# Projections dealt beside the attention in steps of six products, and one weight cast placed behind the first scores

## The chip, the cores and the metric

The kernel runs on one core of one Trainium2 chip. The metric is the device time of one launch in microseconds (us), lower is better. A core has TensorE (PE in the profile, its weight loads PEld), VectorE (DVE), ScalarE (ACT), GpSimd (POOL) and SyncE (SP), which here issues most of the DMAs. Each engine works through its own queue in order, and semaphores join them.

## The reference

One decoder layer over 1024 tokens of width 1024, with 16 learned tokens ahead of them: a feed-forward half step, a mixer with two groups of heads (HGRN2, a gated recurrence, and stick-breaking attention), an output projection, and a second feed-forward half step. All is float32. Cut to what the change touches:

```python
u = rms_norm(h, mix_norm[l]) @ w_in[l]          # 3584 columns
hq, hf, hi, hg, sq, sk, sv = split(u)           # 4 x 512 for HGRN2, 3 x 512 for attention
o_hg = hgrn2(hq, hf, hi, hg, lb, out_gain, valid)
o_sb = stick_breaking(sq, sk, sv, q_gain, k_gain, valid)
h = h + concat([o_hg, o_sb]) @ w_out[l]
# stick_breaking, 8 heads of width 64, blocks of 128 queries, z = q.k / 8:
#   w[t, s] = sigmoid(z_ts) * prod over s < j < t of (1 - sigmoid(z_tj));  out = w @ v
```

## The kernel before, in words

The program has four stages in time: the first feed-forward half (to about 690 us of the trace), the mixer (690 to 1300), the second feed-forward half, and its output. The change lies within the mixer, in the stage that runs the attention, 851 to 1117 us. Every product with a weight is made of three matmuls (lines 249 to 251, tile `proj`): activations and weights are split into a rounded high part and a rest (`xh`, `xl`, `wh`, `wl`), and high times high, high times rest and rest times high are summed. A weight tile `raw` is loaded by a DMA on SP (line 227), cast into `wh` on ACT (line 232), and subtracted into `wl` on DVE (line 234). The raw tiles have two buffers, `wh` and `wl` three each.

The order of TensorE's instructions in this stage is the order in which the Python code emits them. The other engines' order is found by a scheduler from that code and from costs of its own; where the code says `issue_after(x)`, an instruction stands behind `x`.

**The attention** is cut into 32 jobs (8 heads, four pairs of query blocks each, in the order 0, 6, 2, 4), and `braid` gives each job a slot. A job has three kinds of steps. *Scores*, in its own slot: two matmuls (1665, 1666) fill a PSUM tile `z`; ACT makes `keep` and `sig` from it (1667, 1668), DVE runs the product scan over `keep` (1671) and POOL multiplies it into `sig` (1678). *Turns*, two slots later: TensorE transposes `sig` into PSUM tiles `flip` (1515, and 1571 for the meta tokens); ACT casts them into `wu` or `wm` (1643) and DVE subtracts the rest (1644). *Values*, three slots later: pairs of matmuls (1592, 1594) sum into `oacc`. `z` and `flip` have two PSUM banks each, so the third tile of a kind waits until the first is read.

**The fill.** For each slot `braid` adds up the estimated time of the attention steps in it, times 1.22, and draws so much from `hgrn_fill`: the projections of the HGRN2 heads. These go by columns, four per head: v, f, q, g (value, forget gate, query, output gate). v and f are made in four pieces of 256 or 272 tokens, q and g in two of 512. A piece fills one PSUM bank with 24 products, in two steps of twelve. In this stage the fill has one bank alone, the other being lent to a tile `begin` that the scans read. So the first product of a piece waits until the piece before has been read: v by one ACT copy (1148), f by two ACT sigmoids (1154, 1155), q and g by an ACT sigmoid (1162) and a DVE multiply (1163), into staging tiles `st` that have four buffers and are stored by SP.

The weight tile of the next column is loaded and split when the first step of a column is emitted. The first column in this stage is the query of head 0, and with its first step the tile of head 0's output gates is loaded, cast and subtracted. Sixteen steps of the fill (v and f of head 0) run ahead of the stage, 76 in it, and the last four (output gates of head 3) behind it.

Of the kernel before, what the change touches and what calls it, by code (L numbers as in the profile page):

```python
# [15 lines left out]
AF = mybir.ActivationFunctionType  # L16
# [4 lines left out]
P = 128  # L21
D = 1024
KT = D // P
# [26 lines left out]
class Block:  # L50
# [161 lines left out]
            (dst[3], lambda r: kept(3, sub, r[0], r[1])),  # L212
        ]

    def split_w(self, view, parts=None):
        nc = self.nc
        n = int(np.prod(view.shape[1:]))
        if parts is not None:
            got = []
            for i, tag in enumerate(self.w_tags):  # L220
                t = self.wp.tile([P, n], F32R, tag=tag, name="w" + "hl"[i], bufs=self.w_bufs)
                self.last_load = nc.sync.dma_start(t.bitcast(F32), parts[:, i])
                got.append(t)
# [3 lines left out]
        self.last_load = nc.sync.dma_start(to, view)  # L227
        hi = self.wp.tile([P, n], F32R, tag="wh", name="wh", bufs=self.w_bufs)
        if self.split_on_vector:
            nc.vector.tensor_copy(hi, raw)  # L230
        else:
            self.rounded = nc.scalar.copy(hi, raw)
        lo = self.wp.tile([P, n], F32R, tag="wl", name="wl", bufs=self.w_bufs)
        nc.vector.tensor_sub(lo, raw, hi.bitcast(F32))
        return hi, lo

    def col_tile(self, w, col):
        return self.split_w(
            w[:, col : col + P].rearrange("(k p) f -> p k f", p=P), self.parted.get(col)
        )  # L240

    def product(self, ps, w, xh, xl, c0, n, ks=None):
# [888 lines left out]
    def hgrn_fill(self, xh, xl, pool, dst):  # L1131

        nc = self.nc
        plan, cols = self.heads_plan, self.columns_of_heads()
        self.stores, self.level_banks = [], "zo"

        def staged(n):
            return pool.tile([P, 512], F32, tag="st", name="st", bufs=4)[:, :n]

        def use(kind, h, ps, c0, n):  # L1140
            s = slice(c0, c0 + n) if kind in "vf" else slice(c0 - META, c0 - META + n)
            t = staged(n)
            if c0 >= HALVES[1][0] and kind != "g":
                ps = ps[:, ::-1]
                at = s.start + HALVES[1][0] + T - 2 * c0 - n
                s = slice(at, at + n)
            if kind == "v":
                nc.scalar.copy(t, ps)
                with self.tc.issue_after(self.last_load.ins):
                    nc.sync.dma_start(dst[kind][h, :, s], t)  # L1150
                return
            elif kind == "f":
                k = staged(n)
                nc.scalar.activation(t, ps, AF.Sigmoid)
# [5 lines left out]
                nc.sync.dma_start(dst["k"][h, :, s], k)  # L1160
            else:
                nc.scalar.activation(t, ps, AF.Sigmoid)
                nc.vector.tensor_mul(t, t, ps)
            store = lambda: nc.sync.dma_start(dst[kind][h, :, s], t)
            if (kind, h) == plan[-1] and c0 == HALVES[1][0]:
                self.stores.append(store)
            else:
                store()

        kept = {}  # L1170

        def part(i, ci, c0, n, half):
            if ci == 0 and half == 0:
                kept["w"] = self.ahead_w.pop(cols[i])
                for c in cols[i + 1 : i + (3 if i == 0 else 2)]:
                    if c not in self.ahead_w:
                        self.ahead_w[c] = self.col_tile(self.a["w_in"][0], c)
                kept["round"] = self.rounds[cols[1]]
            if half == 0:
                kept["ps"] = self.proj_bank(n)  # L1180
            self.product(
                kept["ps"], kept["w"], xh, xl, c0, n, range(4 * half, 4 * half + 4)
            )
            if half == 1:
                with self.tc.issue_after(kept["round"]) if i == 0 else ExitStack():
                    use(*plan[i], kept["ps"], c0, n)

        for i, (kind, _) in enumerate(plan):
            for ci, (c0, n) in enumerate(PIECES if kind in "vf" else HALVES):
                for half in range(2):  # L1190
                    yield 12 * (n * 0.42 + 13), lambda a=(i, ci, c0, n, half): part(*a)

    def level_bank(self, shape, name):
        self.level_banks = self.level_banks[::-1]
# [451 lines left out]
    def sb_scores(self, pool, qs, ks, b, sigs):  # L1646
        nc = self.nc
        nk = META + P * (b + 1)
        pieces = -(-nk // 512)
        size = -(-nk // pieces)  # L1650
        size += size % 2
        q = qs[:, b * P : (b + 1) * P]
        kept = []

        def piece(s0, n):
            last = s0 + n == nk
            if last:
# [7 lines left out]
            nc.tensor.matmul(z, q, ks[0][:, s0 : s0 + n], start=True, stop=False)  # L1665
            nc.tensor.matmul(z, q, ks[1][:, s0 : s0 + n], start=False, stop=True)
            nc.scalar.activation(keep[:, s0 : s0 + n], z, AF.Sigmoid, scale=-1.0)
            nc.scalar.activation(sig[:, s0 : s0 + n], z, AF.Sigmoid)
            first, end = max(s0, 1), nk + 1 if last else s0 + n
            kv = keep[:, first:end][:, ::-1]  # L1670
            nc.vector.tensor_tensor_scan(
                out=kv, data0=kv, data1=self.begin[:, : end - first] if last
                else self.begin[:, :1].broadcast_to([P, end - first]),
                initial=0.0 if last else keep[:, end : end + 1],
                op0=ALU.mult, op1=ALU.max if last else ALU.bypass,
            )
            if s0 == 0:
                nc.gpsimd.tensor_mul(sig, sig, keep[:, 1 : nk + 1])
# [40 lines left out]
    def braid(self, jobs, fill, share, turn, value):  # L1719


        waiting = []
        owed = 0.0
        at = 0
        while True:
            job = next(jobs, None)
            for lag, steps in zip((0.0, turn, value), job or ()):
                spans = [1.0 if lag == turn else t for t, _ in steps]
                done = 0.0
                for span, (t, f) in zip(spans, steps):  # L1730
                    waiting.append((at + lag + (done + span / 2) / sum(spans), t, f))
                    done += span
            if not waiting:
                break
            now = [x for x in waiting if x[0] < at + 1]
            waiting = [x for x in waiting if x[0] >= at + 1]
            owed += share * sum(t for _, t, _ in now)
            more = []
            while owed > 0:
                step = next(fill, None)  # L1740
                if step is None:
                    break
                more.append(step)
                owed -= step[0]
            now += [(at + (i + 0.5) / len(more), t, f) for i, (t, f) in enumerate(more)]
            for _, _, f in sorted(now, key=lambda x: x[0]):
                f()
            at += 1
# [51 lines left out]
    def run(self):  # L1800
        nc, tc, a = self.nc, self.tc, self.a
# [20 lines left out]
        with ExitStack() as c0:  # L1822
            with ExitStack() as c1:
# [372 lines left out]
                with tc.manual_schedule(engines={nc.tensor.engine}):  # L2196
# [7 lines left out]
                    with ExitStack() as c2:  # L2204
# [216 lines left out]
```

## Time and profile before

| | |
|---|---|
| median of 3 runs | 1938.81 us (1938.69 to 1940.38) |
| the profiled execution's own time | 1938.33 us |
| span of its trace | 1936.6 us |
| DVE busy over the span | 1394.2 us (72%) |
| ACT busy over the span | 847.4 us (44%) |
| POOL busy over the span | 451.4 us (23%) |

The time of the profiled execution and its span differ by 1.73 us, which lies around the trace. A row of the timeline has the start in us, the duration, the engine, the line, the operation, the tile written and the tiles read, the shape, and in brackets the engine's idle time ahead of the instruction with what ended it. Matmuls are pipelined: a row's duration runs over into the next one, so the distance from one start to the next is the cost of a matmul.

### The profile page before, as it was taken

The numbers are of one execution on the slowest core, as the hardware profiler recorded it, in microseconds if no ns is written. First come the engines' busy times: TensorE is split into PE (matmuls) and PEld (weight loads), VectorE is DVE, ScalarE is ACT, GpSimd is POOL, SyncE is SP. The second block draws the span as 40 slices with busy tenths as digits, with TensorE's granted clock in tenths as the row PEclk, the third lists the DMA queues.
The fourth block names the chain that finished last, engine by engine and source line by source line (L and its number), as shares of the span: only waits on it lengthen the run. The fifth ranks groups of instructions, "written<-read, shape, count | busy, mean of one in ns | idle before, by whom it ended". The sixth has DMA issues, their size and how long they took to land.

```text
span 1936.6 us, 30253 instructions
## 1 busy us (share of the span) xinstructions
PE 1915.8 (99%) x10637; PEld 1620.7 (84%) x10637; DVE 1394.2 (72%) x2184; ACT 847.4 (44%) x1712; POOL 451.4 (23%) x625
## 2 busy tenths in 40 slices
PE   9999999999999999999999999999999999999999
PEld 7888888888888888889998988888888888888887
DVE  7977778877678665567777776667577767766774
ACT  7523343334444545356666635433223332344443
POOL 3010100101000003133333342210545544530000
PEclk9999999999999999999999999999999999999999
DMA  7266788757975416765454178646544444479473
GB/s 220 89 175 169 244 280 257 232 199 272 382 238 183 138 42 154 188 182 150 135 155 123 57 267 246 154 185 211 170 128 133 135 127 134 128 251 315 147 233 114
DMA packets 381687, 355.54 MB, mean 184 GB/s; under 512 B 129040, under 2 KB 284560, under 8 KB 381536
## 3 DMA queue, kind: packets, MB, share of 16 engines
q1 hardware_dynamic: 360768, 288.98, 49.3%
q0 software_dynamic: 20768, 64.63, 9.6%
q8 instruction: 84, 1.38, 0.3%
q14 instruction: 67, 0.55, 0.1%
HBM read 237.95 MB, written 115.57 MB: 183 GB/s over the span
## 4 chain that ended last, share of the span: by engine, by line
PE 92%; DVE 3%; DMA 2%; ACT 1%; issue 1%; SPq 0%; POOL 0%; DVEq 0%; POOLq 0%; ACTq 0%
PE o L735 22%; PE qb L452 18%; PE qc L452 12%; PE qa L452 12%; PE proj L249 5%; PE proj L251 5%; PE proj L250 5%; PE flip L1515 2%; PE wo L250 1%; PE wo L251 1%; PE wo L249 1%; PE mq L1014 1%; PE oacc L1594 1%; PE oacc L1592 1%; PE z L1665 1%
## 5 line engine op out<-in xcount | busy, mean ns | idle before, releaser
L452 PE MATMUL qb<-T,wh 128*128 128x512 f32 x1056 | 343.7, 390 | 1.4 <-DVE u L484 1.4
L452 PEld LDWEIGHTS qb<-T,wh 128*128 128x128 f32 x1056 | 198.2, 188 | 45.8 <-issue 3.5
L452 PE MATMUL qa<-B,wh 128*128 128x512 f32 x696 | 227.6, 392 | 0.3 <-ACT B L838 0.2
L362 DVE TENSOR_TENSOR wl<-s,wh 128x512 fp32r<-128x512 f32 x160 | 165.8, 1036 | 69.1 <-ACT wh L360 68.2
L249 PE MATMUL proj<-xh,wh 128*128 128x512 f32 (+2 forms) x640 | 212.7, 332 | 1.1 <-ACT kT L1391 0.6
L735 PE MATMUL o<-t,w 128*128 128x512 f32 x924 | 212.1, 390 | 0.0
L251 PE MATMUL proj<-xl,wh 128*128 128x512 f32 (+2 forms) x640 | 209.3, 327 | 0.7 <-DVE xl L1984 0.7
L735 PE MATMUL o<-parts 128*128 128x512 f32 x924 | 209.6, 389 | 0.0
L250 PE MATMUL proj<-xh,wl 128*128 128x512 f32 (+2 forms) x640 | 208.9, 326 | 0.0
L452 PE MATMUL qb<-T,wl 128*128 128x512 f32 x528 | 205.6, 389 | 0.0
L735 PEld LDWEIGHTS o<-t,w 128*128 128x128 f32 x924 | 172.8, 188 | 37.1 <-issue 0.8
L735 PEld LDWEIGHTS o<-parts 128*128 128x128 f32 x924 | 173.5, 188 | 36.0
L360 ACT CAST wh<-s 128x512 fp32r<-128x512 f32 x160 | 99.5, 622 | 186.6 <-PE qb L452 141.6
L452 PEld LDWEIGHTS qa<-B,wh 128*128 128x128 f32 x696 | 130.5, 188 | 29.2 <-issue 1.0
L360 ACT CAST wh<-raw 128x512 fp32r<-128x512 f32 x120 | 74.4, 621 | 143.2 <-PE qc L452 101.3
L452 PE MATMUL qa<-B,wl 128*128 128x512 f32 x348 | 135.5, 389 | 0.0
L249 PEld LDWEIGHTS proj<-xh,wh 128*128 128x128 f32 x640 | 120.9, 189 | 12.7 <-ACT st L1155 1.2
L251 PEld LDWEIGHTS proj<-xl,wh 128*128 128x128 f32 x640 | 120.9, 189 | 11.8 <-DVE xl L1984 1.2
L250 PEld LDWEIGHTS proj<-xh,wl 128*128 128x128 f32 x640 | 121.1, 189 | 9.2
L452 PEld LDWEIGHTS qb<-T,wl 128*128 128x128 f32 x528 | 99.1, 188 | 20.3
L452 PE MATMUL qc<-T,wh 128*128 128x512 f32 x352 | 115.9, 391 | 0.0
L452 PE MATMUL qc<-B,wh 128*128 128x512 f32 x352 | 114.6, 389 | 0.0
(400 smaller groups left out, 3832.5 us busy)
## 6 DMA issues: line engine op xcount, KB each, us to landing
raw<-in_ffn_w_in_dram SPq DMA_DIRECT2D x176, 256.0 KB, 3.9
raw<-in_ffn_w_out_dram SPq DMA_DIRECT2D x112, 256.0 KB, 4.5
w2in<-both SPq DMA_DIRECT2D x28, 512.0 KB, 4.0
raw<-in_w_in_dram SPq DMA_DIRECT2D x25, 512.0 KB, 4.3
ks<-kD SPq DMA_DIRECT2D x32, 260.0 KB, 4.8
wout<-both SPq DMA_DIRECT2D x16, 512.0 KB, 3.9
wh<-w2in SPq DMA_DIRECT2D x27, 256.0 KB, 3.1
wl<-w2in SPq DMA_DIRECT2D x27, 256.0 KB, 3.3
```

Source lines behind the costliest of these rows:

```text
L249: nc.tensor.matmul(ps, wh[:, s], xs, start=k == 0, stop=False)
L250: nc.tensor.matmul(ps, wl[:, s], xs, start=False, stop=False)
L251: nc.tensor.matmul(ps, wh[:, s], xl[:, k, c0 : c0 + n], start=False, stop=k == nk - 1)
L360: nc.scalar.copy(hi, src)
L362: self.block_lo = nc.vector.tensor_sub(lo, src, hi.bitcast(F32))
L452: nc.tensor.matmul(ps, a[:, k, :], b[:, k, :], start=start and k == 0 and i == 0, stop=k == 3 and i == 2, skip_group_check=True,)
L735: nc.tensor.matmul(banks[bank][m], y[:, m * P : (m + 1) * P], z, start=start and at == 0 and e == 0, stop=q == nq - 1 and e == 2, skip_gro ...
L1014: nc.tensor.matmul(ps[at : at + 32, :], self.xm[:, 4 * h + k, :], got[i, h][:, k, :], start=h == 0 and k == 0, stop=h == 1 and k == 3, til ...
L1515: self.nc.tensor.transpose(ps[:m, j, :], src[:, s0 : s0 + m], self.ident)
L1592: nc.tensor.matmul(o[:, c], vj, w[0], start=j == 0, stop=False, skip_group_check=True)
L1594: nc.tensor.matmul(o[:64, c], vj[:, :64], w[1], start=False, stop=end, skip_group_check=True)
L1665: nc.tensor.matmul(z, q, ks[0][:, s0 : s0 + n], start=True, stop=False)
```

## The change

Two things are changed. First, `hgrn_fill` takes its step from `self.fill_k`. It is four row blocks (twelve products) as before, and two (six products) once `braid` has gone through its second slot; a piece that is begun keeps its step. `braid` spreads the steps of a slot by spans: a step that begins a piece counts two, any other one. The fill ends by the number of row blocks dealt, 92 times 4, which is where it ended before. Second, the load of the first output gates' weight tile stays where it was, but its cast and subtraction are emitted with the second step of the query column, behind the last `sig` that has been emitted by then.

```diff
-    def split_w(self, view, parts=None):
+    def split_w(self, view, parts=None, late=False):
...
         self.last_load = nc.sync.dma_start(to, view)
+        return raw if late else self.split_raw(raw)
+
+    def split_raw(self, raw):
...
-        def part(i, ci, c0, n, half):
-            if ci == 0 and half == 0:
+        def part(i, ci, c0, n, at, m):
+            if ci == 0 and at == 0:
...
-                        self.ahead_w[c] = self.col_tile(self.a["w_in"][0], c)
+                        self.ahead_w[c] = self.col_tile(self.a["w_in"][0], c, i == 2)
                 kept["round"] = self.rounds[cols[1]]
-            if half == 0:
+            if (i, ci, at) == (2, 0, 4):
+                with self.tc.issue_after(self.last_sig.ins):
+                    self.ahead_w[cols[3]] = self.split_raw(self.ahead_w[cols[3]])
+            if at == 0:
                 kept["ps"] = self.proj_bank(n)
...
-                for half in range(2):
-                    yield 12 * (n * 0.42 + 13), lambda a=(i, ci, c0, n, half): part(*a)
+                m = self.fill_k
+                for at in range(0, KT, m):
+                    self.fresh, self.dealt = at == 0, self.dealt + m
+                    yield 3 * m * (n * 0.42 + 13), lambda a=(i, ci, c0, n, at, m): part(*a)
...
-                more.append(step)
+                more.append((*step, 1 + self.fresh))
                 owed -= step[0]
-            now += [(at + (i + 0.5) / len(more), t, f) for i, (t, f) in enumerate(more)]
+            total, done = sum(x[2] for x in more), 0
+            for t, f, span in more:
+                done += span
+                now.append((at + (done - 0.5) / total, t, f))
+            if at == 1:
+                self.fill_k = 2
...
-                        self.braid(jobs, islice(columns, 76), 1.22, 2.0, 3.0)
+
+                        def beside():
+                            while self.dealt < 92 * 4:
+                                yield next(columns)
+
+                        self.braid(jobs, beside(), 1.22, 2.0, 3.0)
+                        self.fill_k = 4
```

The changed file's lines stand 4 to 19 further down: 249 becomes 253, 232 becomes 236, 1515 becomes 1523, 1592 becomes 1600, 1668 becomes 1676. Ahead of the stage and behind it every engine's queue is the same as before. Three places of the queues follow, before and after the change.

**ACT at the start of the stage.** `proj_8545` is the last piece of the forget gate of head 0, `wh_8612` (`wh_8704` after the change) the output gates' weight, `z` the first score tiles. Before:

```order
L232 CAST wh_8612<-raw_8610 128x1024
L1154 ACTIVATE st_8577<-proj_8545 128x256
L1155 ACTIVATE st_8578<-proj_8545 128x256
L1667 ACTIVATE keep_8600<-z_8603 128x144
L1668 ACTIVATE sig_8601<-z_8603 128x144
```

After the change, the same place and then the place where the cast now stands:

```order
L1159 ACTIVATE st_8577<-proj_8545 128x256
L1160 ACTIVATE st_8578<-proj_8545 128x256
L1675 ACTIVATE keep_8600<-z_8603 128x144
L1676 ACTIVATE sig_8601<-z_8603 128x144
...
L1675 ACTIVATE keep_8689<-z_8692 128x400
L1676 ACTIVATE sig_8690<-z_8692 128x400
L236 CAST wh_8704<-raw_8620 128x1024
L1167 ACTIVATE st_8720<-proj_8622 128x512
```

The cast moved from ahead of the last sigmoid pair and all scores to behind eight score tiles, directly ahead of the read of the first query piece.

**DVE about 30 us into the stage.** `wl_9160` is the low part of the weight tile of head 1's forget gate, which is first used some 30 us later; `st_8971` (`st_8979` after) the multiply that reads the first output gate piece. Before:

```order
L1644 TENSOR_TENSOR wu_8863<-flip_8886,wu_8862 128x4x128
L234 TENSOR_TENSOR wl_9160<-raw_9156,wh_9158 128x1024
L1671 SCALAR_TENSOR_TENSOR keep_8914<-keep_8914,begin_8597 128x272
L1644 TENSOR_TENSOR wm01_7922<-flip_8928,wm00_7921 16x256
L1636 TENSOR_TENSOR ot_8837<-oacc_8857,olow_8935 64x256
L1644 TENSOR_TENSOR wu_8942<-flip_8943,wu_8941 128x4x128
L1671 SCALAR_TENSOR_TENSOR keep_8950<-keep_8950,begin_8597 128x457
L1163 TENSOR_TENSOR st_8971<-st_8971,proj_8899 128x512
```

After:

```order
L1644 TENSOR_TENSOR ot_8821<-oacc_8847,olow_8935 64x256
L1652 TENSOR_TENSOR wu_8942<-flip_8943,wu_8941 128x4x128
L1679 SCALAR_TENSOR_TENSOR keep_8956<-keep_8956,begin_8597 128x457
L1652 TENSOR_TENSOR wu_8968<-flip_8969,wu_8967 128x128
L238 TENSOR_TENSOR wl_9160<-raw_9156,wh_9158 128x1024
L1168 TENSOR_TENSOR st_8979<-st_8979,proj_8901 128x512
L1652 TENSOR_TENSOR wu_8942<-flip_8992,wu_8941 128x4x128
```

The subtraction moved from six instructions ahead of the gate's multiply to directly ahead of it. On ACT the cast `wh_9158` moved in the same way, to directly ahead of the gate's sigmoid (L1167), and on SP the load `raw_9156` from behind the load `raw_8893` of the column before it to behind six loads of queries and keys and one store of a query piece.

**TensorE some 118 us into the stage.** `flip_10202` takes the bank of the flip tile two before it, which is `flip_10161` before the change and `flip_10151` after. Before:

```order
L1515 MATMUL flip_10161<-ident_65,sig_9937 128x128 x4
L1592 MATMUL oacc_10109<-wm00_7921,v_9769 128x256
L1594 MATMUL oacc_10109<-wm01_7922,v_9769 64x256
L1665 MATMUL z_10178<-ks_9538,qs_9537 128x392
L1666 MATMUL z_10178<-ks_9539,qs_9537 128x392
L1571 MATMUL flip_10185<-ident_65,sig_9888 16x128
L1571 MATMUL flip_10185<-ident_65,sig_9937 16x128
L1592 MATMUL oacc_10195<-wu_10091,v_9769 128x256
...
L1515 MATMUL flip_10202<-ident_65,sig_10008 128x128 x3
```

After, with six products between (three of them left out, and again the value products ahead of the last row):

```order
L1523 MATMUL flip_10151<-ident_65,sig_9937 128x128 x4
L1600 MATMUL oacc_10103<-wm00_7921,v_9769 128x256
L1602 MATMUL oacc_10103<-wm01_7922,v_9769 64x256
L253 MATMUL proj_10073<-xh_6535,wh_9844 128x512
L254 MATMUL proj_10073<-xh_6535,wl_9846 128x512
L255 MATMUL proj_10073<-xl_6536,wh_9844 128x512
...
L1673 MATMUL z_10178<-ks_9524,qs_9523 128x392
L1674 MATMUL z_10178<-ks_9525,qs_9523 128x392
L1579 MATMUL flip_10185<-ident_65,sig_9894 16x128
L1579 MATMUL flip_10185<-ident_65,sig_9937 16x128
...
L1523 MATMUL flip_10202<-ident_65,sig_10014 128x128 x3
```

Half of the twelve products that stood ahead of the four-fold transpose now stands between it and the tile that takes its bank. At the end of the stage the order changes in the same way: before, the last product of the last query piece of head 3 is followed by eight pairs of value products and two meta transposes, and then by the first product of the stage behind, which takes the same bank; after the change three of these pairs stand between the two.

More of the change, by code (lines that the diff above doesn't have):

```diff
@@ L227, in split_w @@
         self.last_load = nc.sync.dma_start(to, view)
+        return raw if late else self.split_raw(raw)
+    def split_raw(self, raw):
+        nc, n = self.nc, raw.shape[1]
         hi = self.wp.tile([P, n], F32R, tag="wh", name="wh", bufs=self.w_bufs)
@@ L235, in split_w, with col_tile @@
         return hi, lo
-    def col_tile(self, w, col):
+    def col_tile(self, w, col, late=False):
         return self.split_w(
-            w[:, col : col + P].rearrange("(k p) f -> p k f", p=P), self.parted.get(col)
+            w[:, col : col + P].rearrange("(k p) f -> p k f", p=P), self.parted.get(col), late
         )
@@ L1135, in hgrn_fill @@
         self.stores, self.level_banks = [], "zo"
+        self.fill_k, self.dealt = 4, 0
         def staged(n):
@@ L1176, in part @@
                     if c not in self.ahead_w:
-                        self.ahead_w[c] = self.col_tile(self.a["w_in"][0], c)
+                        self.ahead_w[c] = self.col_tile(self.a["w_in"][0], c, i == 2)
                 kept["round"] = self.rounds[cols[1]]
-            if half == 0:
+            if (i, ci, at) == (2, 0, 4):
+                with self.tc.issue_after(self.last_sig.ins):
+                    self.ahead_w[cols[3]] = self.split_raw(self.ahead_w[cols[3]])
+            if at == 0:
                 kept["ps"] = self.proj_bank(n)
[L1181 to L1184, printed above, removed]
+            self.product(kept["ps"], kept["w"], xh, xl, c0, n, range(at, at + m))
+            if at + m == KT:
                 with self.tc.issue_after(kept["round"]) if i == 0 else ExitStack():
@@ L1667, in piece @@
             nc.scalar.activation(keep[:, s0 : s0 + n], z, AF.Sigmoid, scale=-1.0)
-            nc.scalar.activation(sig[:, s0 : s0 + n], z, AF.Sigmoid)
+            self.last_sig = nc.scalar.activation(sig[:, s0 : s0 + n], z, AF.Sigmoid)
             first, end = max(s0, 1), nk + 1 if last else s0 + n
```

## The prediction

> **What bounds the kernel now.** I read the page first, then TensorE in the stage of the change, then the single places where it waits. The page:
>
> ```profile
> span 1936.6 us, 30253 instructions
> PE 1915.8 (99%) x10637; PEld 1620.7 (84%) x10637; DVE 1394.2 (72%) x2184; ACT 847.4 (44%) x1712; POOL 451.4 (23%) x625
> ```
>
> TensorE is the bound throughout. The change takes no instruction away from any engine, so all it can move is TensorE's idle time between 848 and 1121 us. The view of stretches for this one (its length, then each engine's busy time, granted clock, DMA share and rate):
>
> ```profile
> 848.00:1121.00 273.00, 268.25 (x1893) 247.03 (x1892) 205.92 (x345) 180.67 (x466) 98.49 (x141) 1.00 0.46 131
> ```
>
> And the waits of TensorE in it (us in total, times, longest):
>
> ```profile
> PE z L1665 <- ACT sig L1668: 2.0, 5, 0.6
> ...
> PE proj L249 <- DVE st L1163: 0.5, 2, 0.3
> ```
>
> 273.00 less 268.25 is 4.75 us idle. A matmul's row runs over into the next one's time, so each stop costs some 0.16 us more than its idle time: at 970.68 below, the matmul ahead starts at 969.45 and takes 0.12, so TensorE stood for 1.11 where the row says 0.95. Summed in this way, from start to start, all stops of the stage make 7.3 us, or 0.38%. That is all that the change could ever win.
>
> **First change: the cast behind the first scores.** ACT and TensorE at the start:
>
> ```profile
> 847.56 0.32 SPq L1160 DMA_DIRECT2D hg_k<-st  x1
> 849.61 0.43 SPq L1164 DMA_DIRECT2D hg_f<-st  x1
> 850.02 0.39 ACT L1154 ACTIVATE st<-proj 128x256 f32<-128x256 f32 x1 [4.07 <-DMA hg_k<-st]
> 852.69 1.05 ACT L232 CAST wh<-raw 128x1024 fp32r<-128x1024 f32 x1 [1.97 <-DMA raw<-in_w_in_dram]
> 853.65 0.37 ACT L1154 ACTIVATE st<-proj 128x256 f32<-128x256 f32 x1
> 854.18 0.29 ACT L1667 ACTIVATE keep<-z 128x144 f32<-128x144 f32 x1
> 854.70 0.47 PE L1665 MATMUL z<-ks,qs 128*128 128x456 f32 x1 [0.23 <-ACT sig L1668]
> 857.71 0.46 ACT L1667 ACTIVATE keep<-z 128x344 f32<-128x344 f32 x1 [0.41 <-POOL sig L1678]
> 858.57 0.43 PE L1665 MATMUL z<-ks,qs 128*128 128x348 f32 x1 [0.64 <-ACT sig L1668]
> ```
>
> ACT waits 1.97 us for the weight's DMA and casts for 1.05, and behind it queue the last two sigmoids of the forget gate and every score. Without the cast the next limit is the sigmoid's staging tile, which a store must leave first. The store issued at 847.56 let ACT go at 850.02, 2.46 us later; the one issued at 849.61 should do so at 852.07, so the sigmoid of 853.65 can start 1.58 us earlier. TensorE gains less, because it must first finish the twelve products ahead of the 456-wide scores, and then ACT's own pace holds it. Its 0.23 us at 854.70 goes. ACT's 0.41 us for POOL goes too, since the chain from the sigmoid over `begin` and DVE's scan to POOL shifts by 1.58 and more. With what the pipelining hides I take 0.9 us off by 858.57. Some of it is lost at once: the three-fold transpose that now comes up ahead of the products takes a bank that DVE has hardly read, for about 0.1 us. Together **-0.8 us**; the bounds are 0 and -2.0, the latter all of TensorE's waits for `sig` in the stage (first row of the waits).
>
> The cast still has to run. It now stands on ACT in front of the read of the first query piece, while TensorE has twelve products to do (2.7 us at 0.23 each, rows of 865.25 and 865.48 below), which hides 1.05 us. The bound on ACT's side is that 1.05, if the cover is gone.
>
> **A second cast that is moved unasked.** The queues given above show the next load but one, `raw_9156`, with its cast and subtraction directly ahead of the read of head 0's first output gate piece. Before, they were clear of it:
>
> ```profile
> 875.89 1.08 ACT L232 CAST wh<-raw 128x1024 fp32r<-128x1024 f32 x1
> 878.22 1.98 DVE L234 TENSOR_TENSOR wl<-raw,wh 128x1024 fp32r<-128x1024 f32 x1
> 872.17 1.23 DVE L234 TENSOR_TENSOR wl<-raw,wh 128x1024 fp32r<-128x1024 f32 x1
> 881.45 0.56 ACT L1668 ACTIVATE sig<-z 128x456 f32<-128x456 f32 x1
> 883.67 0.60 ACT L1162 ACTIVATE st<-proj 128x512 f32<-128x512 f32 x1 [1.66 <-PE proj L251]
> 967.25 0.39 PE L251 MATMUL proj<-xl,wh 128*128 128x512 f32 x1
> 968.31 0.69 DVE L1163 TENSOR_TENSOR st<-st,proj 128x512 f32<-128x512 f32 x1 [1.63 <-ACT st L1162]
> ```
>
> A query or gate piece is normally read 1.75 us after its last product starts: 967.25 to 968.31 + 0.69 = 969.00. Now ACT comes to the cast about when that product starts, casts for 1.08, then DVE subtracts for 1.23 and multiplies for 0.69: 3.0 us. The order leaves about 2.0 us of other TensorE work until the next piece wants the bank: 0.23 of the product itself, 1.49 of matmuls counted in the order, and 0.3 for two switches from transposes (0.08 at the first matmul, row of 859.88 below, and some at the last transpose). So **+1.0 us**, with bounds 0 and +1.8 (DVE at its 1.98).
>
> **Second change: steps of six.** What it is worth lies in the transposes. Four times they wait for a `flip` bank:
>
> ```profile
> 964.25 0.52 PE L1515 MATMUL flip<-ident,sig 128*128 128x128 f32 x3 [0.63 <-POOL sig L1678]
> 969.45 0.28 PE L1594 MATMUL oacc<-wu,v 128*64 128x256 f32 x1
> 969.87 0.67 DVE L1644 TENSOR_TENSOR wu<-flip,wu 128x512 fp32r<-128x512 f32 x1
> 970.68 0.52 PE L1515 MATMUL flip<-ident,sig 128*128 128x128 f32 x3 [0.95 <-DVE wu L1644]
> 1033.50 0.55 PE L1515 MATMUL flip<-ident,sig 128*128 128x128 f32 x3 [0.31 <-DVE wu L1644]
> 1039.58 0.52 PE L1515 MATMUL flip<-ident,sig 128*128 128x128 f32 x3 [0.15 <-DVE wm L1644]
> ```
>
> In each, only 1.05 to 1.55 us of matmuls (counted in the order) lie between the end of a transpose tile and the start of the second one after it. ACT's cast and DVE's subtraction of a four-fold tile need more. With steps of six the order has 1.7 us at least between any such two, and mostly over 2.4, but for one of 1.05 in the first slots. The four should go: 0.63 + 0.95 + 0.31 + 0.15 + 4 x 0.16 = **-2.7 us**. The bounds are -1.0 (only the longest goes) and -2.9.
>
> Against it, the fill has one bank, and each piece's first product waits for the read of the piece before. A gate or query piece needs 1.80 us from last product to next first product, and in the order of after these gaps are shorter than before for query pieces (1.5 where 2.1 stood), while the two stops for `st` (0.5 us in all above) stay within 0.1. Counted over all pieces, gaps just short of the need add **+0.3 us** (bounds 0 and +1.5, which is some forty pieces by 0.04).
>
> What six cost by themselves is TensorE's switch between kinds of work:
>
> ```profile
> 859.88 0.48 PE L249 MATMUL proj<-xh,wh 128*128 128x512 f32 x1
> 860.20 0.40 PE L250 MATMUL proj<-xh,wl 128*128 128x512 f32 x1
> 865.01 0.40 PE L249 MATMUL proj<-xh,wh 128*128 128x512 f32 x1
> 865.25 0.40 PE L250 MATMUL proj<-xh,wl 128*128 128x512 f32 x1
> 865.48 0.39 PE L251 MATMUL proj<-xl,wh 128*128 128x512 f32 x1
> ```
>
> At 859.88 a step begins behind transposes and its first product takes 0.32; at 865.01 one begins behind value products and takes 0.24, against 0.23 within the step. So only the way out of the transposes costs (0.08), and their runs are as many as before. The 74 added steps (76 become two of twelve and 148 of six) cost nothing: **0**. The Trainium skill, in "Perfetto Trace Analysis", section Matmul Optimizations, asks that matmuls run back to back in batches, because TensorE scales its power with utilization; that speaks against smaller steps. This case's trace does not bear it out so far: the granted clock is 1.00 over the stage (row of the stretch), stops of 0.95 us among it. By the rule smaller steps would add to the sum, by the rows they add nothing.
>
> **The end of the stage.** The last query piece now ends three value pairs ahead of the next piece, which wants the same bank:
>
> ```profile
> 1114.95 0.39 PE L251 MATMUL proj<-xl,wh 128*128 128x512 f32 x1
> 1116.57 0.28 PE L1592 MATMUL oacc<-wu,v 128*128 128x256 f32 x1
> 1117.25 0.39 PE L249 MATMUL proj<-xh,wh 128*128 128x512 f32 x1
> ```
>
> Before, 2.30 us lay between, enough. Now it is 0.23 for the product and 0.68 for the three pairs (1116.57 to 1117.25), 0.91 where 1.80 are needed: **+0.9 us**, between 0 and +0.9.
>
> **The sum.** -0.8 + 1.0 - 2.7 + 0.3 + 0.9 = -1.3 us. Made against the profiled execution of 1938.33 (span 1936.6, 1.73 around it) that is 1937.0; the median of the runs, 1938.81, stands 0.48 above, so 1937.5. A measurement of this kernel can tell about 0.2%, or 3.9 us, from no change; the forecast is within it.
>
> **The rivals.**
>
> *All stops go.* The finer mix also frees the places that I left or charged: the second cast finds ACT early, the end is covered by slack. Then -2.0 - 2.7 = -4.7, 1934.1. For it speaks that ACT and DVE are busy 66% and 75% of the stage (180.67 and 205.92 of 273); against it that the end's bank need is fixed by durations. Chance 0.15.
>
> *The stops only move.* TensorE comes earlier to the next thing that DVE has not read, and of the -2.7 only -1.0 stays: -0.8 + 1.0 - 1.0 + 0.3 + 0.9 = +0.4, 1939.2. DVE's 75% speaks for it; that the new distances are over 1.7 us against it. Chance 0.18.
>
> *The second cast waits for its load* (slower). Before, two weight loads left SP together; now the second stands behind six loads of queries and keys and a store:
>
> ```profile
> 866.32 1.17 SPq L227 DMA_DIRECT2D raw<-in_w_in_dram  x2
> 878.44 2.20 SPq L227 DMA_DIRECT2D raw<-in_w_in_dram  x2
> ```
>
> The page's list of DMAs and the chain of waits have these times to landing:
>
> ```profile
> raw<-in_w_in_dram SPq DMA_DIRECT2D x25, 512.0 KB, 4.3
> 1164.41 7.42 DMA wl<-wout
> ```
>
> I expect its issue near 876, as the query and key loads' bank frees earlier, and landing 4.3 us later, at 880.3; ACT comes to the cast at about 882. If it goes out at 878.44, where SP reached the next loads before, and needs the 7.42 us of the slowest landing shown, it lands at 885.9, and ACT, with all scores and the gate's read behind the cast, loses 3.9 us: -1.3 + 3.9 = +2.6, 1941.4. It decides once issue and landing together pass 882. Chance 0.07.
>
> *Each added step costs* (slower). If the steps of six paid the 0.08 us of the transposes at every begin, that would be 74 x 0.08 = 5.9 us, so -1.3 + 5.9 = +4.6, 1943.4; from 0.02 us a step the kernel is slower than before. The rows of 865.01 speak against it. Chance 0.03. It is where the rule of "Perfetto Trace Analysis" in the Trainium skill would lead.
>
> **How the numbers follow.** The forecast has 0.57; its bounds summed by halves give about 2 us each way. The range 1934.7 to 1940.0 takes it in, with most of the rival that stops move, and leaves out most of the first and the last two. Faster than 0.2% means below 1934.9: most of the first rival and a little of the forecast's edge, 0.12. Slower means above 1942.7: the last rival and part of the late load, 0.05. Within: 0.83.
>
> **What the profile of after would show.** The cast near 860 with no wait for its DMA, the first `keep` before 853, the 348-wide scores near 857.7. No idle over 0.3 ahead of a `flip` after the third slot. A stop of about 1 us ahead of a `proj` some 30 us into the stage, with `wl` just ahead of the gate's multiply on DVE, and one of 0.9 ahead of the first product behind the stage. The span from the first scores to that product, 851.1 to 1117.25 before, should be 1.3 us shorter. I am wrong if steps behind value products take 0.3 us at their first product, if ACT waits for `raw` at the second cast, or if the stops ahead of `flip` stay.

## The result, and the profile after

The changed kernel takes 1942.12 us (median) beside 1938.83 for the kernel before on the same chip: 1.0019 times as long, with an interval of 1.0012 to 1.0025. That is 3.3 us slower, between 2.3 and 4.8. One of its twenty executions took 7417 us and is left out of the ratio. The forecast was 1937.5, so 1.3 us faster, with a range up to 1940.0. Both the sign and the range were wrong.

The head of the page, and then the waits of TensorE in the stage (us in total, times, longest):

```profile
span 1941.1 us, 30248 instructions
PE 1918.1 (99%) x10637; PEld 1620.4 (83%) x10637; DVE 1399.3 (72%) x2184; ACT 850.5 (44%) x1712; POOL 449.4 (23%) x625
```

```profile
PE flip L1523 <- DVE wm L1652: 2.1, 2, 1.4
PE proj L253 <- DVE st L1168: 1.9, 4, 0.8
PE proj L253 <- ACT st L1160: 1.3, 2, 0.9
PE z L1673 <- ACT sig L1676: 1.3, 4, 0.5
PE flip L1523 <- POOL olo L1435: 0.4, 1, 0.4
```

The span grew by 4.5 us. From the first scores to the first product behind the stage it was 851.09 to 1117.25 before, 266.16 us; now it is 850.97 to 1121.41, 270.44. So 4.28 of the 4.5 us lie in the stage. The waits for `sig` fell from 2.0 to 1.3, as forecast. Those of `flip` were to go and are 2.5 where 2.1 stood, and those of `proj` rose from 0.5 to 3.2. They stand in other places than before. The timeline of after at these places (the columns are those of the rows of before):

```profile
850.97 0.23 PE L1673 MATMUL z<-ks,qs 128*128 128x144 f32 x1
...
853.38 0.39 ACT L1159 ACTIVATE st<-proj 128x256 f32<-128x256 f32 x1 [2.42 <-DMA hg_k<-st]
...
857.89 0.42 PE L1673 MATMUL z<-ks,qs 128*128 128x348 f32 x1
860.61 1.06 ACT L236 CAST wh<-raw 128x1024 fp32r<-128x1024 f32 x1
861.89 2.03 POOL L1686 TENSOR_TENSOR sig<-sig,keep 128x1040 f32<-128x1040 f32 x1 [0.89 <-DVE keep L1679]
862.87 2.13 DVE L238 TENSOR_TENSOR wl<-raw,wh 128x1024 fp32r<-128x1024 f32 x1
864.93 0.67 DVE L1168 TENSOR_TENSOR st<-st,proj 128x512 f32<-128x512 f32 x1
865.52 0.41 DVE L1652 TENSOR_TENSOR wm<-flip,wm 16x256 fp32r<-16x256 f32 x1
865.99 0.33 PE L1523 MATMUL flip<-ident,sig 128*128 128x128 f32 x1 [1.43 <-DVE wm L1652]
...
874.54 2.10 DVE L238 TENSOR_TENSOR wl<-raw,wh 128x1024 fp32r<-128x1024 f32 x1 [0.43 <-ACT wh L236]
877.28 0.50 PE L253 MATMUL proj<-xh,wh 128*128 128x512 f32 x1 [0.34 <-DVE st L1168]
...
885.00 1.06 ACT L236 CAST wh<-raw 128x1024 fp32r<-128x1024 f32 x1
886.09 1.23 DVE L238 TENSOR_TENSOR wl<-raw,wh 128x1024 fp32r<-128x1024 f32 x1 [0.19 <-ACT wh L236]
887.23 0.68 DVE L1168 TENSOR_TENSOR st<-st,proj 128x512 f32<-128x512 f32 x1
887.97 0.50 PE L253 MATMUL proj<-xh,wh 128*128 128x512 f32 x1 [0.60 <-DVE st L1168]
...
898.61 1.23 DVE L238 TENSOR_TENSOR wl<-raw,wh 128x1024 fp32r<-128x1024 f32 x1 [0.25 <-ACT wh L236]
900.21 0.33 PE L1523 MATMUL flip<-ident,sig 128*128 128x128 f32 x1 [0.67 <-DVE wm L1652]
...
921.48 1.34 DVE L238 TENSOR_TENSOR wl<-raw,wh 128x1024 fp32r<-128x1024 f32 x1 [0.76 <-ACT wh L236]
925.32 0.42 DVE L1644 TENSOR_TENSOR ot<-oacc,base 64x256 f32<-64x256 f32 x1
925.77 0.41 ACT L1434 CAST ohi<-ot 128x256 fp32r<-128x256 f32 x1 [1.18 <-DVE ot L1644]
926.52 0.41 ACT L1160 ACTIVATE st<-proj 128x272 f32<-128x272 f32 x1
926.98 0.39 PE L253 MATMUL proj<-xh,wh 128*128 128x256 f32 x1 [0.93 <-ACT st L1160]
...
1016.27 0.39 PE L253 MATMUL proj<-xh,wh 128*128 128x256 f32 x1 [0.41 <-ACT st L1160]
1049.94 0.30 PE L1523 MATMUL flip<-ident,sig 128*128 128x128 f32 x1 [0.40 <-POOL olo L1435]
1121.41 0.50 PE L253 MATMUL proj<-xh,wh 128*128 128x512 f32 x1 [0.78 <-DVE st L1168]
```

The pattern to see is a `wl` row on DVE shortly ahead of a TensorE row that has a bracket. The `wl` of 862.87 holds up `wm`, whose bank the transposes of 865.99 want; those of 874.54 and 886.09 hold up a multiply that frees the projection's bank. At 926.98 it seems to work through two engines: the subtraction puts DVE back, `ot` comes late, ACT waits 1.18 us in order at the cast of `ot`, and the forget gate's read queues behind it. The last row is the end of the stage, where no subtraction is near.

### The profile page after: what moved, and what is told of

The parts are those of the page before. It is cut to its first block, busy times and chain, and to the rows that moved or that the text cites. A ratio compares the mean times of both kernels' runs of the same rounds, so it can differ in the third digit from the quotient of the medians.

```text
span 1941.1 us, 30248 instructions
## 1 busy us (share of the span) xinstructions
PE 1918.1 (99%) x10637; PEld 1620.4 (83%) x10637; DVE 1399.3 (72%) x2184; ACT 850.5 (44%) x1712; POOL 449.4 (23%) x625
## 4 chain that ended last, share of the span: by engine, by line
PE 78%; DVE 3%; ACT 2%; DMA 2%; issue 1%; POOL 0%; SPq 0%; DVEq 0%; ACTq 0%; POOLq 0%
PE o L739 22%; PE qb L456 13%; PE qc L456 9%; PE qa L456 9%; PE proj L253 5%; PE proj L255 4%; PE proj L254 4%; PE flip L1523 2%; PE wo L254 1%; PE wo L255 1%; PE wo L253 1%; PE oacc L1602 1%; PE oacc L1600 1%; PE z L1673 1%; PE z L1674 1%
```

## The experiments

Two theories stood at the outset, and a third was made on the way. *Order*: the new stops come from a weight's cast and subtraction standing ahead of a read. *Steps*: each added step costs. *Gap*: with smaller steps too little attention lies between a piece's last product and the next piece's first one, and the fill has one bank. All "stages" below run from the first scores to the first product behind the stage, each in the one execution that was profiled. Sums of stops are from start to start; a stop is marked where its row of the timeline has a bracket, and small where it has none.

**The cast alone.** TensorE, POOL and SP have the order of before; the one cast and subtraction are moved.

```diff
-                more.append((*step, 1 + self.fresh))
+                more.append((*step, 1))
...
-                self.fill_k = 2
+                self.fill_k = 4
```

> The first change alone: the cast behind the first scores, the fill in steps of twelve with the old spread, so that TensorE has the order of the kernel before. Theory (order): the stops of after come from a weight tile's cast and subtraction, or another waiting instruction, that stand on ACT or DVE ahead of the read of a bank that TensorE wants next; a step itself costs nothing. Then the waits for sig shrink as in after (idle 2.0 to 1.3 us), and the subtraction of over 2 us that stood ahead of the 1.43 us stop of after at 865.99 is hidden here, because twelve products stand ahead of that transpose: 0.6 to 0.8 us faster than before, 1938.1. Rival (steps): same here, 0.8 faster, since there are no more steps. Rival (cast): the moved subtraction costs TensorE what it cost in after, 1.4 us and more: 0.6 us slower than before, 1939.4.

Measured: 1938.18 beside 1938.97, ratio 1.0 (0.9991 to 1.0008); stage 266.95, 0.79 more than before's. No change is seen, and the interval holds the forecast of 0.8 us faster as well as the rival's 0.6 slower, so the time doesn't decide between them. The trace does: the stops of `z` fell by 1.3 us (2.99 to 1.70), and one new stop of 1.25 took it back. DVE and TensorE of this kernel:

```profile
861.05 2.13 DVE L238 TENSOR_TENSOR wl<-raw,wh 128x1024 fp32r<-128x1024 f32 x1
863.10 0.67 DVE L1168 TENSOR_TENSOR st<-st,proj 128x512 f32<-128x512 f32 x1
...
863.83 0.50 PE L253 MATMUL proj<-xh,wh 128*128 128x512 f32 x1 [1.09 <-DVE st L1168]
```

The twelve products do hide the transpose, as expected, but the subtraction stands ahead of the multiply too, and the products themselves wait 1.09 us. What the first scores win, the moved subtraction loses.

**The steps alone.** TensorE has the order of after; the cast is where it was before.

```diff
-                        self.ahead_w[c] = self.col_tile(self.a["w_in"][0], c, i == 2)
+                        self.ahead_w[c] = self.col_tile(self.a["w_in"][0], c)
...
-            if (i, ci, at) == (2, 0, 4):
-                with self.tc.issue_after(self.last_sig.ins):
-                    self.ahead_w[cols[3]] = self.split_raw(self.ahead_w[cols[3]])
```

> The second change alone: steps of six with the new spread, the cast where it was. TensorE has the order of after. Theory (order): the stop of 1.43 us at 865.99 goes with the late subtraction, the waits for sig come back (0.8), the other new stops stay: after less 0.8, so 3.7 us slower than before in the span. Rival (steps): every added step costs, so all of the loss is here, and the late cast had only helped: after plus 0.8, 5.3 slower than before. Rival (cast): the late cast is what made it slow: within 1 us of before.

Measured: 1943.29 beside 1938.97, ratio 1.0021 (1.0013 to 1.003); stage 269.57, 0.87 less than after. The stop of 865.99 is gone, the waits for `sig` are 2.1 again, the other stops are after's. So most of the loss in the stage, 3.41 of 4.28 us, comes with the steps. By the medians this kernel is not faster than after; its runs spread from 1940.58 to 1946.36. This run doesn't tell order from steps.

**Even spread.** After, but a step that begins a piece counts one.

```diff
-                more.append((*step, 1 + self.fresh))
+                more.append((*step, 1))
```

> After with the old even spread: a step that begins a piece counts one like any other. Theory (order): the twelve products of the first slots stand ahead of the transpose of 865.99 again, so its 1.43 us goes (1.6 from start to start); in return the gaps ahead of a new piece get shorter, and with them the waits of proj for st grow from 3.2 us idle; by how much is open, I expect 1 to 3. Sum: 0 to 1.5 us slower than after. Rival (steps): as many steps, so as slow as after, within 0.5. Rival (spread): the double span is what brought the new stops: 2 us or more faster than after.

Measured: 1950.93, ratio 1.0062 (1.0049 to 1.0074); stage 278.90. No theory expected 8.8 us over after. Its waits of TensorE:

```profile
PE proj L253 <- DVE st L1168: 6.9, 10, 1.7
PE proj L253 <- ACT st L1160: 2.9, 7, 1.1
PE z L1673 <- ACT sig L1676: 1.4, 4, 0.5
PE proj L253 <- ACT st L1153: 0.5, 2, 0.3
```

Not one `flip` waits, which is what the prediction said steps of six would do. In their place nineteen first products wait for the bank. This made the gap theory.

**Steps of three.**

```diff
-                self.fill_k = 2
+                self.fill_k = 1
```

> After with steps of three products (one row block) from the third slot on in place of six, all else as in after: some 148 steps more. Theory (order): a step costs nothing by itself; the first product behind value products still takes what the next ones take, and the time differs from after only by other stops, within 2 us either way. Rival (steps): after's 4.3 us in the stage came from 74 added steps, some 0.06 each, so 148 more add 8 to 9 us: 1950.

Measured: 1966.19, ratio 1.0139 (1.0123 to 1.0155); stage 293.45. Slower by even more than the rival said, and far outside the 2 us of the order theory, but not for the rival's reason: 29 marked stops of `proj` sum to 27.5 us. The first products of 34 steps of 512 columns behind value products took 0.01 us more than their share (median, longest 0.11). So a step by itself costs next to nothing, and the gap theory fits.

**Spans of three.**

```diff
-                more.append((*step, 1 + self.fresh))
+                more.append((*step, 1 + 2 * self.fresh))
```

> After with a span of three, in place of two, for a step that begins a piece; one bank as in after. Theory (gap): with spans of one, two the waits of proj were 14.1 and 4.5 us; with three they fall to about 2, while the other steps move closer together and some flip waits come back (3.0 to 4): 1 to 2 us faster than after, 1940.5. Rival (order): the stops hang on where casts fall, so any spread is as good as another: within 1 us of after, with other stops.

Measured: 1945.32, ratio 1.003 (1.0019 to 1.0042); stage 271.64, a miss. The marked stops of `proj` fell as expected, 14.05, 4.54, 2.29 us for spans of one, two, three. Those of `flip` rose, 0, 2.97, 7.52. The spread moves stops from one bank to the other, and two is the better of the three.

**Steps of nine, nine and six.**

```diff
+                    m = min(m, KT - at)
...
-                more.append((*step, 1 + self.fresh))
+                more.append((*step, 1 + 0.5 * self.fresh))
...
-                self.fill_k = 2
+                self.fill_k = 3
```

> After with pieces in steps of nine, nine and six products in place of four steps of six, and a span of one and a half for the step that begins a piece. Theory (gap): the share of a piece's attention that lies ahead of a new piece is 1.5 in 3.5, 0.43, against 0.40 in after, 0.25 with the even spread (17.6 us of proj stops) and 0.50 in before; and the other steps stand further apart, 0.29 against 0.20. So less than after on both sides: proj stops some 4 to 5 us (6.3 in after), flip stops 1 to 2 (3.0): 2 to 3 us faster than after, no faster than before. Rival (order): the stops fall where the casts fall, 0 to 2 us from after on either side.

Measured: 1940.95, ratio 1.0013 (1.0004 to 1.0022); stage 268.26. Stops of `proj` 4.4 and of `flip` 2.8 us, the small ones with them. The stage is 2.2 us shorter than after's, as expected, and the median 1.2 us below after's, which is less than expected; the two intervals against before overlap, so the gain is not clear of noise. It is not below before.

**Two banks for the fill,** with `begin` in SBUF: the kernel before, after, and after with the even spread. To make room, all three share one more tile of an attention sum and have a smaller spacing tile.

```diff
...
-                        tag = self.proj_tags[0]
-                        self.proj_tags = [self.proj_tags[1]] * 2
-                        self.begin = self.pproj.tile([P, 512], F32, tag=tag, name="begin", bufs=1)
+                        self.begin = self.att[-1].tile([P, 458], F32, tag="begin", name="begin", bufs=1)
...
-                    self.proj_tags[0] = tag
```

> The kernel before with the same two banks, the control. All theories: before has 1.0 us of marked waits of proj, so at most 1 us faster, 1938; if the scans that read begin from SBUF take longer, this kernel shows how much, up to 3 us slower.

> After, with the tile begin in SBUF in place of the PSUM bank that it borrows, so that the fill has two banks by turns (to make room, the 1 KB tile of the upper half of an attention sum is shared, begin is cut to the 458 columns that are read, and a spacing tile is 8 columns in place of 24). TensorE's order is that of after. Theory (gap): the loss of after is the wait of a piece's first product for the read of the piece before; 4.5 us of marked waits for st and 1.1 above before's in small ones go, the flip waits (3.0) and those for sig stay: stage 270.4 - 5 = 265.4, about 1 us faster than before, 1938. Rival (order): the casts ahead of the reads are the loss in themselves; the flips and scores behind them wait in place of the projections: within 1.5 us of after. Unknown: what a scan costs that reads begin from SBUF; the kernel before with the same move shows it.

> Steps of six with the even spread (11 us slower than before with one bank: 19 waits of proj, 14 us, no wait of flip at all), and the same two banks. Theory (gap): all waits of proj go, and the flips still do not wait, so the stage has only the waits for sig (2.3) left: 278.9 - 14.1 - 2.5 = 262.3, 3.9 us less than before, 1935. Rival (steps): the steps of six themselves cost, so at least half of the 11 us stays: over 1943. Rival (order): casts now hold up the flips in place of the projections: 1938 to 1942.

Measured: before 1943.78 (1.0025, 1.0016 to 1.0035), after 1944.01 (1.0022, 1.0012 to 1.0032), even 1938.55 (0.9996, 0.9987 to 1.0005); stages 271.74, 271.53 and 267.07. The control lost 4.9 us: the scans took 124 us of DVE between 848 and 1118 where 97 stood, and `flip` waited for DVE instead. So the number for before missed by the price of the scans. After gains nothing against the control: no `proj` waits in it, but `flip` stops of 8.4 us stand in their place, the longest of them 3.17 us idle with half clock behind it (last section). The even steps missed their 1935 by 3.6 us, less than that price. Against the control, which pays it too, they are 5.2 us faster, and no `proj` waits. With one bank they were 12.0 us slower than before. So it is the one bank that turns the finer, even mix from a gain into a loss. Two banks with `begin` still in PSUM were not tried: in this kernel `begin` holds the bank that the fill would need.

**Reads first.** After, with the reads of the projections' bank at high priority.

```diff
-                    use(*plan[i], kept["ps"], c0, n)
+                    with self.tc.high_priority():
+                        use(*plan[i], kept["ps"], c0, n)
```

> After with the reads of the projection bank (sigmoids, copy, multiply and their stores) at high priority in the scheduler; it moves some ten places on ACT and DVE, TensorE's order stays. Theory (order): where a cast or a transpose's cast stood ahead of a read, the read now goes first; the waits of proj fall from 4.5 us to 3 or less, while those of flip grow by less; 0.5 to 2 us faster than after. Theory (gap): the read of a piece takes as long as before once it begins, and what is put behind it makes the flips wait: within 1 us of after.

Measured: 1944.35, ratio 1.0032 (1.002 to 1.0045), but the profiled stage is 269.16, 1.3 shorter than after's, with `proj` at 2.5 us of wait and the waits for `sig` at 2.0. Five runs from 1941.59 to 1947.39 and a profile that points the other way leave the time of this one inconclusive. Its trace speaks for the order theory at two places: the subtractions of 874.54 and 886.09 now stand behind the multiply, and the first products that waited at 877.28 and 887.97 no longer wait. The scores of 864.50 wait 1.21 us, where 0.33 stood in after.

**No subtraction.** After, and the kernel before, without the 13 `wl` of the stage. The second of each three products reads `wh` again, so the rest of these weights is left out of the result; TensorE has as many products as before.

```diff
+        if getattr(self, "begin", None) is not None:
+            return hi, hi
...
+                        self.begin = None
```

> After without the 13 subtractions wl of the stage: the second product of each three takes the high part of the weight a second time, so the rest of the weights is left out of these projections; TensorE has as many products in the same order, DVE has 19.5 us less. Theory (order, in its narrow form): five new stops of after have a weight's subtraction of 1.2 to 2.1 us ahead of the read that TensorE waits for (865.99, 877.28, 887.97, 900.21, 1049.94: 1.59 + 0.49 + 0.88 + 0.83 + 0.55 = 4.3 us from start to start); they go, and the stage falls from 270.4 to 266, a little below before. Theory (gap): the gaps of after are too short for the reads with or without the subtraction; half of it at most goes, 268.5, and the waits at 926.98, 1016.27, 1067.37 and 1121.41 stay.

> The kernel before without the same subtractions, the control: its stops at 964.25, 970.68, 1033.50 and 1039.58 stand ahead of transposes in slots where I see no weight's subtraction next to the read. Theory (order): little changes, 0 to 1 us faster than before, stage 265.2 to 266.2, so that after without them is no slower than this. Theory (gap): both lose alike, and after without them stays 2 us or more above this.

Measured: after 1937.49 (0.9993, 0.9984 to 1.0001), before 1937.29 (0.9996, 0.9987 to 1.0005); stages 265.96 and 266.53. By these times the difference between the two kernels is gone. The waits of TensorE, first after without, then before without:

```profile
PE proj L255 <- DVE st L1170: 1.6, 3, 0.8
PE z L1675 <- ACT sig L1678: 1.3, 4, 0.5
PE proj L255 <- ACT st L1162: 0.4, 1, 0.4
```

```profile
PE z L1667 <- ACT sig L1670: 1.7, 4, 0.6
PE flip L1517 <- DVE wu L1646: 1.3, 2, 1.0
PE flip L1517 <- POOL sig L1680: 0.6, 1, 0.6
PE proj L251 <- DVE st L1165: 0.5, 2, 0.3
PE flip L1517 <- DVE wm L1646: 0.2, 1, 0.2
```

After's stage is 4.48 us shorter by it, before's 0.37 longer. But the run of before without subtractions had half clock for 3.41 us among its first scores (last section), which none of the other three had. Behind it all four ran at full clock. From the 328-wide scores to the end, before takes 252.87 us (864.38 to 1117.25) and after 257.65 (863.76 to 1121.41), so 4.78 more; without subtractions they take 252.24 (866.32 to 1118.56) and 253.17 (863.49 to 1116.66), so 0.93 more.

Of the five stops that I had named, four went (865.99, 877.28, 900.21, 1049.94: 3.46 us). The fifth stayed, 0.93 in place of 0.88. This run can't tell what the subtraction does there, since ACT's cast now comes late for another reason, its load:

```profile
883.33 1.05 ACT L236 CAST wh<-raw 128x1024 fp32r<-128x1024 f32 x1 [0.57 <-DMA raw<-in_w_in_dram]
885.64 0.50 PE L255 MATMUL proj<-xh,wh 128*128 128x512 f32 x1 [0.66 <-DVE st L1170]
```

A sixth that I hadn't named, 926.98, fell from 1.09 to 0.24. Together 4.3 us. The scheduler also moved a few other instructions when the subtractions went. None of these moves lies shortly ahead of the four stops, but at the sixth `ot` now stands ahead of `wm` (0.41 us) on DVE, so part of the 0.85 may be due to that move.

The account is then: without the subtractions, steps of six win 3.0 us at the transposes (2.63 + 0.45 of marked and small stops of `flip` in the one from before, 0.04 in the one from after) and lose 2.8 at the one bank (`proj` 3.00 + 1.84 against 0.98 + 1.06), so little is left. The subtractions cost 0.6 us in before's order and 4.5 in after's, by the stretches above.

## Why the prediction was wrong, by its own steps

- **First cast, -0.8.** The scores did what was said: the stops of `z` fell by 0.83 us, and the cast ran at 860.61 without waiting for its DMA. The reason given was partly off, since `keep` began at 854.03 and not before 853: the sigmoid ahead of it waited 2.42 us for a store. The step failed where it said that the cast's only bound was ACT's 1.05 us. With the cast goes its subtraction on DVE, 2.13 us beside POOL, and no term had it. It cost 1.59 at 865.99, and 1.25 at 863.83 where the cast was moved alone.
- **Second cast, +1.0.** Right: 0.88 at 887.97 (0.11 of it the last transpose's own time), with `wl` and the multiply in the order that was read off. It was the only one of the stage's subtractions that was looked for.
- **Waits ahead of `flip`, -2.7.** This step failed most. The four old stops did go, but three new ones of 2.97 us came, 1.59 of them the stop of 865.99 that the first cast's subtraction made. The step compared each gap with what a transpose tile's own cast and subtraction need. DVE's queue held a weight's subtraction there as well, and without it no `flip` waits.
- **One bank, +0.3 (0 to 1.5).** Mis-sized: 877.28, 926.98 and 1016.27 cost 2.16 us and small stops 0.64 more than before, less 0.41 for one that went: 2.4. About half of it, 0.49 at 877.28 and 0.85 at 926.98, hangs on subtractions.
- **End of the stage, +0.9.** Right: 0.94 at 1121.41.
- **Switches, 0.** Right, and shown by the steps of three.
- **The sum.** By these terms the stage grew by 3.7 us (-0.8 + 0.9 + 0.3 + 2.4 + 0.9, the 1.59 counted with `flip`) where -1.3 was forecast and 4.28 was measured. The other 0.6 us was not assigned.
- **The rivals.** "The stops only move" came nearest, with DVE late for what TensorE comes to earlier, but it didn't name the weights' subtractions, and its price was +0.4 where 4.3 was measured. The load of the second cast was not late (its cast at 885.00 has no bracket).

## What to carry to other kernels

When an order changes, list every long instruction of the reading engines, casts and subtractions for later tiles above all, and look at what each one now stands ahead of; a gap is long enough only against the read plus whatever is queued before it. Before making a mix finer, look at every buffer whose distances shrink by it: evenly spread steps of half the size, 12.0 us slower with one bank and 5.2 faster with two, halved the gap in front of the one bank, and spreading them to widen that gap took the cover from the transposes' banks. Check an instruction that moves along with another as a term of its own.

## What the runs showed of the hardware

A scan that reads both operands from SBUF waited for POOL. Rows of before, and of the control with `begin` in SBUF (each DVE, then POOL):

```profile
886.75 0.86 DVE L1671 TENSOR_TENSOR_SCAN keep<-keep,begin 128x345 f32<-128x345 f32 x1
886.43 1.81 POOL L1678 TENSOR_TENSOR sig<-sig,keep 128x912 f32<-128x912 f32 x1 [4.60 <-DVE keep L1671]
```

```profile
889.77 2.20 DVE L1669 TENSOR_TENSOR_SCAN keep<-keep,begin 128x345 f32<-128x345 f32 x1
889.44 1.80 POOL L1676 TENSOR_TENSOR sig<-sig,keep 128x912 f32<-128x912 f32 x1 [5.14 <-DVE keep L1669]
```

Beside the same multiply of POOL, the scan takes 0.86 us with `begin` in PSUM and 2.20 with it in SBUF; there it ends at 891.97, 0.73 us after the multiply's end at 891.24. The subtraction `wl`, which reads two SBUF tiles, takes 1.23 us alone (886.09 of after) and 2.13 beside a multiply (862.87). The Trainium skill says in "SBUF — State Buffer", section SBUF: two separate sides, that DVE with two SBUF inputs and GpSimd lock a shared port pair for a whole instruction, the other one blocking; these rows agree, with DVE as the one that came second and waited.

TensorE's clock fell to half within the stage in three of the runs. Stretches of the kernel with steps of three (the last column but two is the granted clock):

```profile
889.00:891.40 2.40, 0.00 (x0) 0.00 (x0) 2.40 (x5) 0.00 (x0) 0.00 (x0) 0.78 0.09 17
891.40:894.00 2.60, 2.54 (x7) 2.17 (x8) 0.79 (x2) 0.27 (x1) 0.00 (x0) 0.50 0.90 287
898.00:905.00 7.00, 6.33 (x41) 5.42 (x39) 4.16 (x7) 4.38 (x12) 3.71 (x5) 1.00 0.01 2
```

A stop of 3.68 us ended there at 891.46. The mean of 0.78 over the first stretch means 1.06 us at half clock, so the clock fell near 890.34, some 2.6 us into the stop. Matmuls of 512 columns took 0.43 us in place of 0.23 until 897. In after with two banks a stop of 3.17 us, ended at 868.06, did the same, 1.7 us into it (0.78 over 864.90 to 868.00). Single stops of 1.81 us (867.51 of the even steps with two banks) and 1.77 (904.32 of after with two banks) did not. But the clock also fell in the kernel before without subtractions, where the marked stops ahead were of 0.58, 0.48 and 0.30 us:

```profile
855.30:858.69 3.39, 2.03 (x8) 0.95 (x7) 3.08 (x7) 3.20 (x10) 0.95 (x3) 1.00 0.72 200
858.69:862.10 3.41, 3.41 (x10) 2.60 (x11) 3.20 (x4) 2.52 (x8) 1.91 (x3) 0.50 0.98 233
```

So the length of one stop does not decide it alone; what does was not tested. The Trainium skill, in "TensorE: Matmul & The Clock Gate", Part 1, puts the drop to half clock behind an idle window of about 3.4 us; here it came 1.7 and 2.6 us into a stop, and once with TensorE busy for 2.03 of the 3.39 us ahead.
